# The slot gates' chain moved behind the first expert's w3 products, in both MoE layers

## The chip, the cores and the metric

The kernel runs on one core of a Trainium2 chip. Five engines work from instruction queues of their own and wait for each other through semaphores: the PE (TensorE, matrix products, with weight loads shown apart as PEld), the DVE (VectorE), ACT (ScalarE), POOL (GpSimd) and SP (SyncE, which issues transfers). The metric is the device time of one launch in microseconds (us), and lower is better.

## What is computed

Two layers of a diffusion backbone over 256 latent tokens and 256 context tokens of width 1024, in float32. Each layer ends with a mixture of 16 experts, which is the part that matters here. A router picks two of the 16 experts for each token, and gives it two gate weights:

```python
w = jnp.take_along_axis(scores, expert_idx, axis=-1)
w = w / jnp.sum(w, axis=-1, keepdims=True)
gate = jnp.sum(jax.nn.one_hot(expert_idx, N_EXPERTS) * w[..., None], axis=1)
out = jnp.zeros_like(tok)
for e in range(N_EXPERTS):
    hid = jax.nn.silu(tok @ w1[e]) * (tok @ w3[e])
    out = out + gate[:, e:e + 1] * (hid @ w2[e])
```

w1 and w3 are 1024x512 for each expert, w2 is 512x1024. Layer 0 routes 512 tokens, layer 1 only the 256 latent ones.

## The kernel before

**Slots.** The router sorts the tokens into slots: up to 128 tokens for each expert in layer 0, and for each group of four experts in layer 1. The tables `tok` (which token sits in a slot) and `gw` (its gate weight, a column for each expert) have one row for each slot. `tok` is made at once, since the gathers need it. `gw` is made by a function `R["weights"]()`, which the kernel calls later: a chain of small DVE operations (L972 to L985 in layer 0, L1388 to L1402 in layer 1) that ends in a bf16 table, `wv` or `wb`. Then come small PE products of that table with the one-hot slot matrices (8 in layer 0, `tbw` at L1018; 2 in layer 1, L1430; "the gate product" below) and three DVE operations that add up the parts into `gw`. If an expert or a group had more than 128 tokens, a branch ahead of this would run; it isn't taken with these inputs.

**One expert.** POOL gathers the expert's token rows from memory into a buffer `xg` (there are two, used in turn). The PE transposes them (eight transposes, `tsp`), and ACT and DVE copy the result into two parts, `xh` and `xl`, the value rounded for the PE's fast float32 form and what is left over. Weights come in 1 MB loads into six slots (`raw`); each is split in the same way in two halves, `whi` by ACT (L176) and `wlo` by DVE (L178), into six sets of slots, which are taken again when the PE is through with them. I count these split halves in the order of their use: 1 to 4 are w1 of expert 0, 5 to 8 its w3, 9 and 10 the first half of expert 1's w1, 11 to 14 expert 0's w2, 15 and 16 the second half of expert 1's w1. Every product is then three, hi by hi, hi by lo and lo by hi (`mm3`, L318 to L320), so that a split half feeds six. Of the hidden tiles the DVE makes `g`, which is transposed and split into `gh` and `gl` and multiplied with w2.

**Order.** The code is written expert by expert: the second half of w1, w3 in two halves, the next expert's transposes, `g`, the first half of the next expert's w1, then w2. What stands in each engine's queue is not that order but what a scheduler makes of it when the kernel is built: it plays the program through with costs of its own, and puts an instruction in front of an earlier one where that one would wait. On the chip the queues are then fixed. `issue_after(ins)` keeps the instructions of a block that run on the engine of `ins` behind it in that queue; it sets no wait. `mm_last` is the last PE product that `mm3` has issued.

**Around the change.** In layer 0 the gathers for experts 0 and 1 are issued ahead of the branch, and between them POOL issues four weight loads:

```python
first = self.e_gather(0)
with self.tc.issue_after(first.ins):
    self.ld = nc.gpsimd
    self.prefetch([("moe_w3", (0, 0), 4 * i, 4, 0, 512) for i in range(2)])
    self.prefetch([("moe_w2", (0, 0), 0, 4, 512 * n, 512) for n in range(2)])
    self.ld = nc.sync
    second = self.e_gather(1)
```

All other weight loads go through SP's queue. In layer 1 the first group's tokens are picked by a product on the PE instead of a gather, and four experts share them.

Of the kernel before, what the change touches and what calls it, by code (L numbers as in the profile page):

```python
# [110 lines left out]
class Net:  # L111
# [566 lines left out]
    def moe(self, layer, NT):  # L678
        nc = self.nc
        assert layer == 0  # L680
        with ExitStack() as es:
            rp = self.pool(es, f"moe_r{layer}", 1)
            psp = self.pool(es, f"moe_tp{layer}", 3, space=PSUM)
            hps = self.pool(es, f"moe_h{layer}", 3, space=PSUM)
            yps = self.pool(es, f"moe_y{layer}", 2, space=PSUM)
            fin = [self.ada_mm(1, c, (hps, "h"), psp) for c in self.fill]
            self.prefetch([("moe_w1", (0, 0), 4 * i, 4, 0, 512) for i in range(2)])
            R = self.route(layer, NT, rp, psp)
            with self.tc.issue_after(R["dve"].ins):
                for f in fin:  # L690
                    f()
            self.branch_hint(layer, R)
            self.g2 = [self.mod_bc(rp, layer, G2, i, tag=f"g2{i}") for i in range(NT // 2)]
            ep = self.pool(es, f"moe_e{layer}", 2)
            self.xs = [[ep.tile([128, 8, 128], F32R, name=f"{n}{i}", bufs=1) for n in ("xh", "xl")] for i in range(2)]
            self.facc = ep.tile([128, 2, D], F32, name="facc", bufs=1)
            last = R["dve"]
            after = lambda: (es2.enter_context(self.tc.issue_after(i.ins)) for i in (last, self.rt_act))
            with ExitStack() as es2:
                list(after())  # L700
                xg = self.experts_setup(layer, NT, R, ep, psp, hps, yps)
# [7 lines that stand above are left out]
            with self.tc.issue_after(second.ins):  # L709
                rv = nc.values_load(R["ovf"][0:1, 0:1], min_val=0, max_val=1)  # L710
            self.overflow(rv, self.facc[:, 0], self.facc[:, 1])
            with ExitStack() as es2:
                list(after())
                self.dve_mark, self.act_mark = self.mark()
                es2.enter_context(self.tc.issue_after(self.dve_mark.ins))
                es2.enter_context(self.tc.issue_after(self.zeroed.ins))
                self.act_mark = self.e_tr(0)
                self.e_gather(len(xg))
                self.e_hid(0, "moe_w1", 0)
                R["weights"]()  # L720
                self.expert(0)
            for e in range(1, 16):
                self.expert(e)
            self.hx.close()
            self.moe0_tail(ep, psp, hps)
# [339 lines left out]
    def expert(self, e):  # L1065
        nc, X = self.nc, self.X
        layer, NT, ep, psp, hs, R, T = (X[k] for k in ("layer", "NT", "ep", "psp", "hs", "R", "T"))
        gw = R["gw"][:, e:e + 1]
        self.e_hid(e, "moe_w1", 1)
        self.e_hid(e, "moe_w3", 0)  # L1070
        self.e_tr(e + 1)
        self.e_gather(e + 1 + len(X["xg"]))
        self.e_hid(e, "moe_w3", 1)
        g = ep.tile([128, 512], F32, tag="g", name="g")
        nc.scalar.activation(g, hs[e, "moe_w1"], AF.Silu)
        nc.vector.tensor_tensor(g, g, hs[e, "moe_w3"], ALU.mult)
        gh = ep.tile([128, 4, 128], F32R, tag="gh", name="gh")
        gl = ep.tile([128, 4, 128], F32R, tag="gl", name="gl")
        self.transpose_split(g, 4, gh, gl, psp)
        self.e_hid(e + 1, "moe_w1", 0)  # L1080
        if e < 15:
            y = ep.tile([128, D], F32, tag="y", name="y")
        else:
            S = ep.tile([128, T], F32R, name="S", bufs=1)
            with self.tc.issue_after(self.dve_mark.ins):
                self.onehot(S, NT, R["tokf"][:, e:e + 1])
            yh = ep.tile([128, D], F32R, name="yh", bufs=1)
            yl = ep.tile([128, D], F32R, name="yl", bufs=1)
            X["y"] = S, yh, yl
            wts = [self.weight(("moe_w2", (layer, e), 0, 4, 512 * n, 512)) for n in range(2)]  # L1090
            self.add_sum(2)
        for n in range(2):
            ns = slice(512 * n, 512 * n + 512)
            wt = wts[n] if e == 15 else self.weight(("moe_w2", (layer, e), 0, 4, 512 * n, 512))
            ps = X["yps"].tile([128, 512], F32, tag="y", name="y_ps")
            for k in range(4):
                self.mm3(ps, (gh[:, k], gl[:, k]), self.wk(wt, k), k == 0, k == 3)
            if e < 15:
                nc.scalar.activation(y[:, ns], ps, AF.Copy, scale=gw)  # L1099
            else:  # L1100
                nc.scalar.activation(yh[:, ns], ps, AF.Copy, scale=gw)
                nc.vector.scalar_tensor_tensor(yl[:, ns], ps, gw, yh[:, ns].bitcast(F32), ALU.mult, ALU.subtract)
        if e < 15:
            nc.gpsimd.indirect_dma_start(out=self.F[:, :],  # L1104
                                         out_offset=bass.IndirectOffsetOnAxis(ap=R["tok"][:, e:e + 1], axis=0),
                                         in_=y, in_offset=None, bounds_check=T - 1, oob_is_err=False,
                                         compute_op=ALU.add)
# [352 lines left out]
    def moe1(self):  # L1460
        nc = self.nc
        NT = 2
        with ExitStack() as es:
# [4 lines left out]
            R = self.route1(NT, rp, psp)  # L1468
# [23 lines left out]
            with ExitStack() as es2:  # L1492
                list(after())
                self.dve_mark, self.act_mark = self.mark()
                es2.enter_context(self.tc.issue_after(self.dve_mark.ins))
                self.split_group0(tps)
                for g in range(1, 4):
                    self.gather(xg[g - 1], self.xd, R["tok"][:, g:g + 1], 256)
                self.e_hid(0, "moe_w1", 0)
                R["weights"]()  # L1500
                self.expert1(0)
            for g in range(4):
                nc.gpsimd.memset(hg[g], 0.0)
# [5 lines left out]
    def expert1(self, e):  # L1509
        nc, X = self.nc, self.X  # L1510
        ep, psp, hs, R = (X[k] for k in ("ep", "psp", "hs", "R"))
# [3 lines left out]
        if j == 2 and grp < 3:  # L1515
            xh, xl = X["xs"][(grp + 1) % 2]
            self.transpose_split(X["xg"][grp], 8, xh, xl, psp)
        self.e_hid(e, "moe_w3", 1)
        g = ep.tile([128, 512], F32, tag="g", name="g")
        nc.scalar.activation(g, hs[e, "moe_w1"], AF.Silu)  # L1520
# [196 lines left out]
```

## Time and profile before

| | before |
|---|---|
| device time, three runs | 1286.89, 1287.11, 1289.53 us (median 1287.11) |
| profiled execution, its own time | 1290.84 us |
| its span in the trace | 1289.0 us |
| PE busy | 1203.7 us (93%) |
| DVE busy | 941.8 us (73%) |
| ACT busy | 755.6 us (59%) |
| mean granted clock of the PE | 0.976 of full |
| bytes moved by DMA | 340.60 MB, mean 264 GB/s |

The experts of layer 0 take from about 331 us to 620 us in the span, those of layer 1 from about 978 us to the end. A busy PE is one with a product under way; the granted clock tells at which speed. Products overlap in the pipeline, so the time that one takes away from the next is the distance between two starts and not the duration in the row.

### The profile page before, as it was taken

To read this page: it belongs to the slowest core of one execution; us is meant where nothing else is said; L and a number is where in the kernel's file an instruction comes from. 1 tells how busy PE (TensorE), PEld (TensorE's weight loads), DVE (VectorE), ACT (ScalarE), POOL (GpSimd) and SP (SyncE) were. 2 spreads that over 40 slices of the span, in tenths; PEclk is the share of its full clock that TensorE was granted. 3 is DMA by queue.
4 is the path that set the end of the run, shared out by engine and by line. 5 is a ranking of instruction groups with operands and counts; after the bars stand their busy time and mean duration, and the time that the engine had idled before them with its cause. 6 is when DMAs were issued, how large, how long until landed. Compare 5 with 4: busy or idle time off the path is not lost. (4 is left out here: it accounts for less than half of the span.)

```text
span 1289.0 us, 18819 instructions
## 1 busy us (share of the span) xinstructions
PE 1203.7 (93%) x7093; PEld 946.8 (73%) x7093; DVE 941.8 (73%) x1601; ACT 755.6 (59%) x1122; POOL 124.5 (10%) x126
## 2 busy tenths in 40 slices
PE   4999999898699999999979999999997999999995
PEld 3777666566588888777668888898776788877673
DVE  4755666866698989888897554554657899888985
ACT  3753555723488888778544433343435777777663
POOL 1010102300111112111000000000004000000020
PEclk8999999999799999999989999999998999999998
DMA  9666774342899999999883445432749999889980
GB/s 348 254 238 244 270 256 153 106 166 102 332 354 373 365 363 365 359 362 347 299 326 111 147 157 199 154 119 98 270 174 359 369 369 367 336 334 344 336 335 9
DMA packets 60885, 340.60 MB, mean 264 GB/s; under 512 B 10252, under 2 KB 14860, under 8 KB 24144
## 3 DMA queue, kind: packets, MB, share of 16 engines
q1 hardware_dynamic: 46656, 303.07, 62.4%
q0 software_dynamic: 11392, 31.81, 7.6%
q10 hardware_dynamic: 2736, 4.41, 1.0%
q8 instruction: 59, 0.97, 0.3%
q14 instruction: 42, 0.34, 0.1%
HBM read 333.74 MB, written 18.40 MB: 273 GB/s over the span
## 5 line engine op out<-in xcount | busy, mean ns | idle before, releaser
L178 DVE TENSOR_TENSOR wlo<-raw,whi 128x1024 fp32r<-128x1024 f32 x471 | 558.8, 1221 | 114.2 <-ACT whi L176 113.0
L176 ACT ACTIVATE whi<-raw 128x1024 fp32r<-128x1024 f32 x476 | 481.2, 1054 | 106.8 <-PE qk_ps L319 24.5
L319 PE MATMUL h_ps<-wlo,xh 128*128 128x512 f32 x512 | 208.6, 407 | 4.5 <-DVE wlo L178 4.3
L318 PE MATMUL h_ps<-whi,xh 128*128 128x512 f32 x512 | 206.1, 403 | 3.3 <-ACT xh L1457 2.4
L320 PE MATMUL h_ps<-whi,xl 128*128 128x512 f32 x512 | 206.1, 402 | 0.1
L319 PEld LDWEIGHTS h_ps<-wlo,xh 128*128 128x128 f32 x512 | 97.6, 191 | 38.4 <-DVE wlo L178 17.6
L318 PEld LDWEIGHTS h_ps<-whi,xh 128*128 128x128 f32 x512 | 97.9, 191 | 26.0 <-ACT xh L1457 2.6
L320 PEld LDWEIGHTS h_ps<-whi,xl 128*128 128x128 f32 x512 | 97.6, 191 | 21.3 <-DVE xl L675 0.7
L275 PE MATMUL ada_ps<-raw,cT 128*32 128x128 f32 x1536 | 53.8, 276 | 2.1 <-DMA raw<-in_ada_w 2.1
L319 PE MATMUL y_ps<-wlo,gh 128*128 128x512 f32 (+1 forms) x136 | 53.5, 394 | 0.4 <-DVE wlo L178 0.3
L318 PE MATMUL y_ps<-whi,gh 128*128 128x512 f32 (+1 forms) x136 | 53.0, 391 | 0.7 <-ACT gh L674 0.7
L320 PE MATMUL y_ps<-whi,gl 128*128 128x512 f32 (+1 forms) x136 | 52.6, 395 | 0.1
L275 PEld LDWEIGHTS ada_ps<-raw,cT 128*32 128x32 f32 x1536 | 41.4, 110 | 13.9 <-issue 9.2
L319 PE MATMUL y<-wlo,gh 128*128 128x512 f32 x124 | 49.1, 396 | 0.4 <-DVE wlo L178 0.3
L318 PE MATMUL y<-whi,gh 128*128 128x512 f32 x124 | 49.2, 397 | 0.2 <-ACT gh L674 0.2
L320 PE MATMUL y<-whi,gl 128*128 128x512 f32 x124 | 48.4, 400 | 0.9 <-DVE gl L675 0.8
L1104 POOL DMA_INDIRECT moe_sum<-y,tok x15 | 28.1, 1877 | 158.1 <-ACT y L1099 158.1
L674 ACT ACTIVATE gh<-tsp 128x512 fp32r<-128x512 f32 x32 | 19.1, 596 | 41.4 <-PE tsp L671 41.2
L318 PE MATMUL qk_ps<-xhi,whi 128*128 128x512 f32 x96 | 39.4, 410 | 0.0
L319 PE MATMUL qk_ps<-xlo,whi 128*128 128x512 f32 x96 | 38.7, 403 | 0.0
L320 PE MATMUL qk_ps<-xhi,wlo 128*128 128x512 f32 x96 | 38.3, 399 | 0.0
L1604 POOL DMA_INDIRECT out_dram<-hg,tok x4 | 10.6, 2638 | 268.0 <-DVE hg L1598 218.4
(441 smaller groups left out, 2391.9 us busy)
## 6 DMA issues: line engine op xcount, KB each, us to landing
raw<-in_moe_w SPq DMA_DIRECT2D x188, 1024.0 KB, 7.6
raw<-in_ada_w SPq DMA_DIRECT2D x48, 1024.0 KB, 5.3
raw<-in_ret_w_in SPq DMA_DIRECT2D x24, 1024.0 KB, 5.7
raw<-in_mixab_w_in SPq DMA_DIRECT2D x10, 1024.0 KB, 5.6
raw<-in_ret_w_out SPq DMA_DIRECT2D x8, 1024.0 KB, 4.9
raw<-in_mixab_w_out SPq DMA_DIRECT2D x4, 1024.0 KB, 8.2
raw<-in_moe_w POOLq DMA_DIRECT2D x4, 1024.0 KB, 11.0
bias<-in_rpb ACTq DMA_DIRECT2D x12, 256.0 KB, 5.6
```

Of the source, the lines that this page charges most:

```text
L176: self.nc.scalar.activation(hi, r, AF.Copy)
L178: eng.tensor_tensor(lo, r, hi.bitcast(F32), ALU.subtract)
L275: mm = nc.tensor.matmul(ps[32 * j:32 * j + 32, 0:128], self.cT[:, kk, :], raw[:, k, 128 * j:128 * j + 128], start=(kk == 0), stop=(kk == 7 ...
L318: mm(out, lh, rh, start=first, stop=False)
L319: mm(out, lh, rl, start=False, stop=False)
L320: self.mm_last = mm(out, ll, rh, start=False, stop=last)
L674: i = nc.scalar.activation(hi[:, b0:b0 + w], tv, AF.Copy)
L1104: nc.gpsimd.indirect_dma_start(out=self.F[:, :], out_offset=bass.IndirectOffsetOnAxis(ap=R["tok"][:, e:e + 1], axis=0), in_=y, in_offset=N ...
L1604: self.nc.gpsimd.indirect_dma_start(out=self.out[:, :], out_offset=bass.IndirectOffsetOnAxis(ap=idx, axis=0), in_=x, in_offset=None, bound ...
```

## The change

The call of `R["weights"]()` moves. In layer 0 it stood behind the first half of expert 0's w1 and now stands behind its w3 and expert 1's transposes; in layer 1 it stood at the same place and now stands between the two halves of w3. Its PE products are kept behind the last product that was written before it. Nothing is added and nothing is left out.

```diff
@@ moe, layer 0
                 self.e_hid(0, "moe_w1", 0)
-                R["weights"]()
                 self.expert(0)
@@ expert, layer 0
         self.e_tr(e + 1)
         self.e_gather(e + 1 + len(X["xg"]))
         self.e_hid(e, "moe_w3", 1)
+        if e == 0:
+            with self.tc.issue_after(self.mm_last.ins):
+                R["weights"]()
@@ moe1, layer 1
                 self.e_hid(0, "moe_w1", 0)
-                R["weights"]()
                 self.expert1(0)
@@ expert1, layer 1
+        if e == 0:
+            with self.tc.issue_after(self.mm_last.ins):
+                R["weights"]()
         self.e_hid(e, "moe_w3", 1)
```

The queues of the built kernels show what the scheduler makes of it. The PE's queue at the start of layer 0's experts, before; `xg_3540` and `xh_3535` belong to expert 0, `xg_3541` and `xh_3537` to expert 1, and the first gap holds 45 more products of expert 0:

```order
L671 MATMUL tsp<-cst,xg_3540 128x128 x8
L318 MATMUL h_ps<-whi,xh_3535 128x512
L319 MATMUL h_ps<-wlo,xh_3535 128x512
L320 MATMUL h_ps<-whi,xl_3536 128x512
...
L1018 LDWEIGHTS os_0_3473
L1018 MATMUL tbw<-wv_10198,os_0_3473 128x48
...
L671 MATMUL tsp<-cst,xg_3541 128x128 x8
L318 MATMUL h_ps<-whi,xh_3537 128x512
L319 MATMUL h_ps<-wlo,xh_3537 128x512
L671 MATMUL tsp<-cst,g 128x128 x4
```

The same place of the changed kernel; the gap before the seven transposes holds 33 more products of expert 0, the next one its last 12, and 12 products of expert 1's w1 stand in the third:

```order
L671 MATMUL tsp<-cst,xg_3540 128x128 x8
L318 MATMUL h_ps<-whi,xh_3535 128x512
L319 MATMUL h_ps<-wlo,xh_3535 128x512
L671 MATMUL tsp<-cst,xg_3541 128x128
L320 MATMUL h_ps<-whi,xl_3536 128x512
...
L671 MATMUL tsp<-cst,xg_3541 128x128 x7
...
L318 MATMUL h_ps<-whi,xh_3537 128x512
...
L319 MATMUL h_ps<-wlo,xh_3537 128x512
L1017 LDWEIGHTS os_0_3473
L1017 MATMUL tbw<-wv_10276,os_0_3473 128x48
...
L671 MATMUL tsp<-cst,g 128x128 x4
```

The gate product has moved behind 14 products of expert 1, the last two of which need split half 15. The transposes of expert 1's tokens, which stood behind it, have moved up: the first is now third from expert 0's first product, the other seven stand behind its first half of w3.

The DVE's queue of the changed kernel at the same stretch, from expert 0's last split of w3 (the last of the six) to the left-over part `gl` of expert 0's `g`; the first gap holds the splits 9 and 10 and expert 1's `xl`, the second the splits 12 to 15 with gate operations between them, and the third two more pairs of a one-hot row and a gate addition and the fourth one-hot row:

```order
L178 TENSOR_TENSOR wlo<-raw,whi 128x1024 x6
L971 TENSOR_TENSOR t_0_3466<-of_3442,sc 128x64 x2
...
L1078 TENSOR_TENSOR g<-g,h_ps 128x512
L974 RECIPROCAL one_10262<-one_10262 128x4
L178 TENSOR_TENSOR wlo<-raw,whi 128x1024
...
L984 TENSOR_TENSOR wv_10276<-of_3442,wb_10270 128x8x16
L178 TENSOR_TENSOR wlo<-raw,whi 128x1024
L791 TENSOR_SCALAR S<-cb,tokf_3481 128x128
L1020 COPY gw_3472<-tbw 128x16
...
L675 TENSOR_TENSOR gl<-tsp,gh 128x512
```

Before, the gate operations stood between the splits 2 to 10, the last of them in front of `g` and of all splits of w2; now most of them stand between the splits 11 to 15, behind `g`. The one-hot `S` of expert 15 (four operations) stood some ten splits later.

The PE's queue in layer 1 at the gate product of the changed kernel; `h_ps` are here products of expert 1:

```order
L319 MATMUL h_ps<-wlo,xh_16066 128x512
L1432 LDWEIGHTS os_1_16015
L1432 MATMUL tbw<-wb_17565,os_1_16015 128x48
...
L320 MATMUL h_ps<-whi,xl_16067 128x512
...
L671 MATMUL tsp<-cst,g 128x128 x4
...
L318 MATMUL y_17634<-whi,gh 128x512
L319 MATMUL y_17634<-wlo,gh 128x512
```

The gate product stands seven products later than before (behind the second product of split half 16 and not behind the first of half 15), and the first w2 product (`y`) also has seven more products in front of it than before.

## Rows read from the trace of the kernel before

**Rows 1.** Table of 20-us stretches: busy us of each engine, PEclk, DMA share, GB/s.

```profile
350.00:370.00 20.00, 19.06 (x80) 15.17 (x79) 17.09 (x19) 14.95 (x20) 4.13 (x4) 0.84 0.95 332
370.00:390.00 20.00, 20.00 (x94) 16.20 (x93) 19.21 (x23) 17.10 (x21) 3.67 (x3) 1.00 1.01 370
...
590.00:610.00 20.00, 20.00 (x91) 15.39 (x90) 17.44 (x17) 16.10 (x20) 1.69 (x1) 1.00 1.00 352
```

**Rows 2.** PE timeline, layer 0: start, duration, instruction, [idle before <- releaser].

```profile
332.88 0.79 PE L318 MATMUL h_ps<-whi,xh 128*128 128x512 f32 x1
...
334.06 0.79 PE L320 MATMUL h_ps<-whi,xl 128*128 128x512 f32 x1
...
345.49 0.40 PE L320 MATMUL h_ps<-whi,xl 128*128 128x512 f32 x1
348.79 0.37 PE L1018 MATMUL tbw<-wv,os 128*128 128x48 bf16 x8 [2.91 <-DVE wv L985]
349.13 1.53 PE L671 MATMUL tsp<-cst,xg 128*128 128x128 f32 x8
351.60 0.80 PE L318 MATMUL h_ps<-whi,xh 128*128 128x512 f32 x1 [0.94 <-ACT xh L674]
...
352.62 1.05 PE L671 MATMUL tsp<-cst,g 128*128 128x128 f32 x4
...
354.33 0.63 PE L319 MATMUL h_ps<-wlo,xh 128*128 128x512 f32 x1
354.75 0.63 PE L320 MATMUL h_ps<-whi,xl 128*128 128x512 f32 x1
...
356.44 0.39 PE L318 MATMUL h_ps<-whi,xh 128*128 128x512 f32 x1
356.67 0.40 PE L319 MATMUL h_ps<-wlo,xh 128*128 128x512 f32 x1
...
357.14 0.40 PE L318 MATMUL y_ps<-whi,gh 128*128 128x512 f32 x1
...
368.33 1.03 PE L671 MATMUL tsp<-cst,xg 128*128 128x128 f32 x8
```

**Rows 3.** POOL timeline at the end of layer 0's routing, columns as before.

```profile
326.57 2.17 POOL L157 DMA_DIRECT2D raw<-in_moe_w  x4
329.04 1.05 POOL L1026 DMA_INDIRECT xg<-xd,tok  x1 [0.30 <-issue]
```

**Rows 4.** DMA issues of 328.95 to 331 us: what, median us to landing.

```profile
xg<-xd,tok POOLq DMA_INDIRECT x1, 19.9
```

**Rows 5.** DMA queues, 340 to 349 us: packets, MB, share of 16 engines.

```profile
q1 hardware_dynamic: 424, 3.10, 82.1%
q0 software_dynamic: 193, 0.65, 18.2%
```

**Rows 6.** ACT timeline, layer 0.

```profile
346.23 4.83 ACT L176 ACTIVATE whi<-raw 128x1024 fp32r<-128x1024 f32 x5
350.97 1.07 ACT L674 ACTIVATE xh<-tsp 128x512 fp32r<-128x512 f32 x2
353.71 0.60 ACT L674 ACTIVATE gh<-tsp 128x512 fp32r<-128x512 f32 x1 [1.68 <-PE tsp L671]
355.42 1.06 ACT L176 ACTIVATE whi<-raw 128x1024 fp32r<-128x1024 f32 x1 [1.11 <-PE h_ps L320]
```

**Rows 7.** DVE timeline, layer 0.

```profile
348.45 0.28 DVE L985 TENSOR_TENSOR wv<-of,wb 128x128 bf16<-128x128 f32 x1
...
354.95 4.70 DVE L178 TENSOR_TENSOR wlo<-raw,whi 128x1024 fp32r<-128x1024 f32 x4
```

**Rows 8.** PE timeline, layer 1.

```profile
998.23 0.80 PE L319 MATMUL h_ps<-wlo,xh 128*128 128x512 f32 x1 [2.12 <-DVE wlo L178]
...
1003.44 0.50 PE L318 MATMUL y<-whi,gh 128*128 128x512 f32 x1 [0.22 <-ACT gh L674]
```

**Rows 9.** DVE timeline, layer 1.

```profile
996.97 1.21 DVE L178 TENSOR_TENSOR wlo<-raw,whi 128x1024 fp32r<-128x1024 f32 x1
```

## Prediction

> **What bounds the kernel now.** I read the stretch table first, then the timeline of the PE at the two places where the diff moves something, and last the timelines of the engines and queues that the PE waits for there. In the expert part of layer 0 the table shows the PE busy for all of 20 us at a granted clock of 1.00 in each of the twelve stretches from 370 us to 610 us (the first and the last are in [rows 1]). A product of 128x512 then comes every 0.23 us (356.44 to 356.67), and no later stretch of this part has slack in which a delay could be caught up. So whatever the PE loses at the start of the experts moves the end by as much, and whatever it gains there counts in full.
>
> What it loses there today is in its timeline [rows 2]. The 48 products of expert 0's w1 and w3 run from 332.88 to 345.9. Then the gate product waits 2.91 us for the last gate operation of the DVE. The eight transposes for expert 1 follow at 349.13, there are 0.94 us of waiting for their copy, and expert 1's products start at 351.60 0.42 us apart (354.33 to 354.75), until about 356.4. That is the lower of the PE's two clocks, 1.2 GHz and not 2.4; the stretch from 350 to 370 has a granted clock of 0.84. The products of w2 start at 357.14.
>
> It looks as if the gate chain costs 2.9 us. The second wait is hidden behind it. Expert 1's tokens come by a gather that POOL issues at 329.04, behind four weight loads of 1 MB that it issued from 326.57 [rows 3]; the gather lands 19.9 us after its issue [rows 4], at 348.9. The transposes at 349.13 could not have started before. So the gate product and the transposes become ready within 0.2 us of each other, and taking the gates away would leave the PE at the same place at the same time.
>
> **What the change does, step by step.** The number of instructions is the same; the order is what changes. On the PE in layer 0 the gate product goes behind 14 products of expert 1, as meant. But the transposes for expert 1, which stood behind the gate product, move up with the gap that it left: the first of the eight now stands behind only two of expert 0's products. The PE takes its instructions in order. It gets there at 334.06 (the start of today's third product) and must wait for the gather, with 46 products behind it that ran during the flight until now.
>
> *When the gather lands.* From 340 to 349 us its queue (q0) moves its last 0.65 MB while SP's queue (q1) moves 3.10 MB [rows 5], 0.417 MB per us together. SP loads into a slot when the DVE has split what was in it. Held PE means held slots: the fourth of SP's loads needs splits 7 and 8, which need slots that the stopped products hold. Of the 3.10 MB at most 1.05 MB (one load) is then missing, which is worth 1.05 / 0.417 = 2.5 us at most: landing at 346.4 if all of it was in the gather's way, 348.9 if none. The missing load is the last of the four, so I take 348.0. The Trainium skill, "DMA: Bandwidth & Descriptors", section on queues, rings and completion order, says that each DMA engine takes turns between the queues that have work, a packet at a time. With half of the engines' rate the 0.65 MB would be through at 343.1 in this kernel today, and the change would cost 4.9 us less than I say; the trace has q0 at 18.2% against 82.1%, so equal turns do not give the gather equal bytes.
>
> *From the landing T to the first w2 product, layer 0.*
> - PE: 46 products and 8 transposes. After a wait the products run at 0.43 us for some 4.8 us (351.60 to 356.4): 11 in that time, 35 at 0.233 are 8.2, and the transposes 0.9 (1.03 for eight at 368.33): T + 13.9. ACT's splits fit in: it makes one in 0.97 (4.83 for five), each when the product set six before has freed the slot, as the wait at 355.42 shows [rows 6].
> - DVE: only when w3's products are done can it multiply g (0.6). Behind that stand five weight splits (4.70 for four, so 1.175 each: 5.9) with the gate operations between them, an estimated 1.3 in all (nine, the last 0.28 long, overlapping in part) [rows 7]. The last gate operand is ready at T + 13.9 + 0.6 + 7.2 + 0.2 for the hand-over = T + 21.9. The PE has twelve products of expert 1 and one more to do meanwhile (3 us), and stands for 4 to 5 us. This is a new wait of the kind that the edit was to remove.
> - Then the gate product and the four transposes of g at half clock (1.05 at 352.62) and their copy (0.60 at 353.71): 2.1. The first w2 product comes at T + 24.0.
>
> With T = 348.0 that is 372.0, where today it is 357.14: +14.9. The new order has done 16 of expert 1's w1 products by then, not 12: -0.9. About six w2 products run at half clock after the new wait: +1.1. Sum for layer 0: **+15.1**, with bounds +13.5 (T = 346.4) and +16.0 (T = 348.9). Loads cause no wait of their own: the slots fill while the PE stands.
>
> *Layer 1.* Here the transposes are not touched. The PE waits 2.12 us at 998.23 for one weight split [rows 8], which the DVE starts at 996.97 behind interleaved gate operations [rows 9]. Four of these, an estimated 0.1 us each, move behind it: it starts some 0.3 earlier, and so does the PE. Afterwards the gate product, now behind seven more products, delays the three additions and the next split: the PE waits 0.7 for that split and 0.2 for the copy of g. The first w2 product would come at 1005.4 where it came at 1003.44, with 7 more products behind it (1.6): +0.3. One later split of expert 1's w3 stands one place further back on ACT, which may cost up to 1.2 more, or nothing. Bounds -0.3 and +1.5; I take **+0.5**.
>
> **Sum.** +15.1 + 0.5 = +15.6 us. Against the profiled execution (1290.84 us, span 1289.0) that is 1306.4. It stands 3.7 above the median of the three timed runs, 1287.11, and the sum against that gives 1302.7; I say 1303.
>
> **The rivals.**
> - *The gather lands early.* If the stop on the PE frees the DMA engines far more than by one load, or the two queues share evenly (0.65 MB at half of 0.417 is 3.1 us from 340), T is about 343.1, and the sum is 4.9 less, +10.7: 1298. For it: 0.65 MB is little. Against it: q0's share as above, and three of SP's loads are issued all the same.
> - *The PE isn't held at the transposes,* since they are passed or the tokens are there at 334. The 48 products and the transposes are then done at 346.8, but the copies for expert 1 stand behind three splits on ACT (2.9 us from 346.23, and 1.07 for the copies) and end at 350.2; its products run at half clock to 354.9; the DVE's row of five splits begins at 351.1, and 7.8 later the last gate operand comes, at 358.9, the first w2 product at 361.0. With the -0.9 and +1.1 of above that is +4.0 in layer 0, so 1291.6. The Trainium skill, "TensorE: Matmul & The Clock Gate", in its table of specifications, says that TensorE's queue reorders in part, pulling weight loads ahead of products that are under way; read as letting ready products past, it would give this time. The trace speaks against that reading: during the 2.12 us wait of 998.23 the next product, whose operands were there, did not run.
> - *Faster.* The wait of 2.91 at the gate product goes, with the 0.94 behind it, and the half clock after it (11 products at 0.19 more: 2.1), and nothing takes its place: 1287.1 - 5.9 = 1281. It decides itself at one point, the last gate operand: it must be ready when the PE has done 62 products, near 350. Today it is ready at 348.7, with the splits of w2 behind it; in the new order they stand in front.
> - *A longer hold.* On the DVE the four one-hot operations of expert 15 come up in front of the gate additions and of the copy that the w2 products need. In the built program the first of them waits for a transfer on POOL's queue. If that is expert 3's gather, which can be issued some 13 us after T when its buffer is transposed, and it takes 19.9 us like the one before, it holds the DVE until T + 33 and not T + 23 or so, the w2 products 9 us longer: 1312.
> - *Nothing,* within 0.2%: some of the above cancel. No single row gives it.
>
> That the change doesn't take effect is excluded by the order rows.
>
> **How the numbers follow.** My forecast, T between 346.4 and 349: 0.70. Early gather 0.10, PE not held 0.07, faster 0.04, longer hold 0.06, nothing 0.03. The first two lie in 1297 to 1308, with 2 us for the half-clock stretches and layer 1 on either side; that leaves 0.20 out. A difference of 0.2% (2.6 us) is about what a measurement of this kernel tells from none. Faster by more than that 0.04, within it 0.03, slower 0.93.
>
> **What would show it.** In the timeline of the changed kernel: two products, then a PE wait of 12 to 15 us that ends with the transfer of expert 1's tokens; a second one of 4 to 5 us before the gate product, ended by the DVE; the first w2 product at 370 to 373; nearly the same busy stretches after it, some 15 us later; and in layer 1 less than 2 us either way. The prediction is wrong if the first transposes run at 334, if the second wait is missing, or if a later stretch of layer 0 makes up for several us, which would mean that the PE was not the bound there.

## The result and the profile after

The changed kernel takes **1304.66 us** (median of three runs, 1303.7 to 1306.42), where the kernel before took 1287.11. The ratio is 1.0128, with an interval of 1.0114 to 1.0143, so 14.7 to 18.4 us more. The forecast was 1303. The profiled execution took 1304.66 us, span 1302.8.

The table of 20-us stretches of the changed kernel, with the columns of [rows 1], shows where the time goes. The first stretch has 12 PE instructions, transposes among them, where the stretch from 330 to 350 of the kernel before had 70; from 390 on the PE is again busy for all of each stretch until 630.

```profile
330.00:350.00 20.00, 3.53 (x12) 2.63 (x13) 8.34 (x9) 3.09 (x4) 0.00 (x0) 0.50 0.87 361
...
390.00:410.00 20.00, 20.00 (x94) 16.09 (x93) 18.63 (x20) 16.82 (x21) 3.15 (x2) 1.00 1.00 359
```

The PE's timeline of the changed kernel, layer 0, is the answer to [rows 2]:

```profile
330.80 1.94 PE L671 MATMUL tsp<-cst,xg 128*128 128x128 f32 x8 [5.37 <-DMA xg<-xd,tok]
332.58 0.79 PE L318 MATMUL h_ps<-whi,xh 128*128 128x512 f32 x1
333.17 0.63 PE L319 MATMUL h_ps<-wlo,xh 128*128 128x512 f32 x1
349.47 0.45 PE L671 MATMUL tsp<-cst,xg 128*128 128x128 f32 x1 [15.67 <-DMA xg<-xd,tok]
349.57 0.78 PE L320 MATMUL h_ps<-whi,xl 128*128 128x512 f32 x1
...
362.91 0.39 PE L320 MATMUL h_ps<-whi,xl 128*128 128x512 f32 x1
...
370.75 0.58 PE L319 MATMUL h_ps<-wlo,xh 128*128 128x512 f32 x1 [4.39 <-DVE wlo L178]
371.13 0.54 PE L1017 MATMUL tbw<-wv,os 128*128 128x48 bf16 x8
...
373.28 0.79 PE L318 MATMUL y_ps<-whi,gh 128*128 128x512 f32 x1
...
384.17 1.03 PE L671 MATMUL tsp<-cst,xg 128*128 128x128 f32 x8
```

Two products run, then one transpose waits 15.67 us for expert 1's tokens, and the product behind it (349.57), whose operands are those of the two before and their left-over part, waits with it. The last of expert 0's 48 products starts at 362.91. The second wait, 4.39 us, stands one product ahead of the gate product and is for a weight split (`wlo`), not for a gate operand; the gate product runs right behind it. At equal work, 24 w2 products and 36 of expert 1, the next transposes start at 384.17, 53.37 us after the first ones at 330.80. Before, these were 368.33 and 331.10 [rows 2], 37.23 us apart. So layer 0 loses **16.1 us** by there.

The DVE's timeline of the changed kernel shows the second wait from the other side. The operations from L971 to L984 are the gates.

```profile
352.75 1.23 DVE L178 TENSOR_TENSOR wlo<-raw,whi 128x1024 fp32r<-128x1024 f32 x1 [14.11 <-ACT whi L176]
...
363.34 0.69 DVE L1078 TENSOR_TENSOR g<-g,h_ps 128x512 f32<-128x512 f32 x1
...
367.71 0.28 DVE L984 TENSOR_TENSOR wv<-of,wb 128x128 bf16<-128x128 f32 x1
...
369.48 1.22 DVE L178 TENSOR_TENSOR wlo<-raw,whi 128x1024 fp32r<-128x1024 f32 x1
370.61 0.28 DVE L984 TENSOR_TENSOR wv<-of,wb 128x128 bf16<-128x128 f32 x1
370.81 1.22 DVE L178 TENSOR_TENSOR wlo<-raw,whi 128x1024 fp32r<-128x1024 f32 x1
```

The DVE stood for 14.11 us as well, because no split slot came free: ACT, which makes the other half of each split first, waited for the PE to get through with the set in use (ACT's timeline of the changed kernel):

```profile
351.66 1.06 ACT L176 ACTIVATE whi<-raw 128x1024 fp32r<-128x1024 f32 x1 [16.39 <-PE h_ps L320]
```

From `g` on the DVE works without a gap, and the split that ends at 370.7 is the one for which the PE waits; the last gate operand follows 0.2 us later, while the PE is in that product.

In layer 1 the PE's timeline of the changed kernel answers to [rows 8]:

```profile
994.42 0.50 PE L318 MATMUL h_ps<-whi,xh 128*128 128x512 f32 x1 [3.50 <-ACT xh L1459]
...
1013.40 0.50 PE L319 MATMUL h_ps<-wlo,xh 128*128 128x512 f32 x1 [2.19 <-DVE wlo L178]
1013.74 0.39 PE L320 MATMUL h_ps<-whi,xl 128*128 128x512 f32 x1
...
1017.24 0.50 PE L319 MATMUL h_ps<-wlo,xh 128*128 128x512 f32 x1 [0.64 <-issue]
...
1019.56 0.50 PE L318 MATMUL y<-whi,gh 128*128 128x512 f32 x1
```

### The profile page after: what moved, and what is told of

It is laid out like the page before. It is cut to its first block, busy times and chain, and to the rows that moved or that the text cites. A ratio compares the mean times of both kernels' runs of the same rounds, so it can differ in the third digit from the quotient of the medians.

```text
span 1302.8 us, 18824 instructions
## 1 busy us (share of the span) xinstructions
PE 1202.7 (92%) x7093; PEld 946.4 (73%) x7093; DVE 942.3 (72%) x1601; ACT 756.3 (58%) x1122; POOL 125.2 (10%) x126
## 5 line engine op out<-in xcount | busy, mean ns | idle before, releaser
L319 PEld LDWEIGHTS h_ps<-wlo,xh 128*128 128x128 f32 x512 | 97.1, 190 | 41.6 <-DVE wlo L178 20.1
L671 PE MATMUL tsp<-cst,xg 128*128 128x128 f32 x152 | 22.5, 281 | 21.0 <-DMA xg<-xd,tok 21.0
```

Source lines behind the costliest of these rows:

```text
L319: mm(out, lh, rl, start=False, stop=False)
L671: nc.tensor.transpose(tp[:, 128 * b:128 * b + 128], src[:, 128 * (b0 + b):128 * (b0 + b) + 128], self.ident)
```

## The experiments

Eleven kernels, in three sets; each set has runs of the kernel before of its own, with medians of 1288.62, 1287.54 and 1287.37 us (single runs from 1283.6 to 1293.4).

**E1: the hold without the gates' move.** Layer 1 as before; in layer 0 only expert 1's transposes are written earlier.

```diff
@@ before: moe
                 self.e_hid(0, "moe_w1", 0)
+                self.e_tr(1)
+                self.e_gather(3)
                 R["weights"]()
@@ expert
-        self.e_tr(e + 1)
-        self.e_gather(e + 1 + len(X["xg"]))
+        if e:
+            self.e_tr(e + 1)
+            self.e_gather(e + 1 + len(X["xg"]))
```

> Before, with one thing changed in layer 0: expert 1's transposes are written ahead of the gates, so that the PE's queue has the first of them behind two of expert 0's products, as in the changed kernel; the gates stay early on the DVE, ahead of g, and layer 1 is as before. Theory of the prediction (the hold at the transposes is the larger half, the gates behind the splits the smaller): the PE waits 15 to 16 us for the gather at the third product, there is no second wait of 4 us, the first w2 product comes near 368, and the time is 1297 to 1300. Rival (the gates' place on the DVE makes most of the cost): 1287 to 1292. Rival (the hold makes all of it): 1303 to 1305.

Measured: 1299.59, ratio 1.0082 (1.006 to 1.0103), so 11.0 us more than before by the medians, 7.7 to 13.3 by the interval. The PE's timeline of E1 has the first wait, a little shorter than the 15 to 16 us expected, and no other behind it:

```profile
347.13 0.45 PE L671 MATMUL tsp<-cst,xg 128*128 128x128 f32 x1 [14.12 <-DMA xg<-xd,tok]
...
364.72 0.41 PE L318 MATMUL y_ps<-whi,gh 128*128 128x512 f32 x1
```

By the medians the hold, without a gate moved, makes about two thirds of the loss (11.0 of 17.55). Both rivals are out.

**E2: the gates' move without the hold.** The changed kernel, with expert 1's transposes kept behind expert 0's last product.

```diff
@@ after: expert
-        self.e_tr(e + 1)
-        self.e_gather(e + 1 + len(X["xg"]))
+        if e:
+            self.e_tr(e + 1)
+            self.e_gather(e + 1 + len(X["xg"]))
         self.e_hid(e, "moe_w3", 1)
+        if e == 0:
+            with self.tc.issue_after(self.mm_last.ins):
+                self.e_tr(1)
+            self.e_gather(3)
         if e == 0:
             with self.tc.issue_after(self.mm_last.ins):
                 R["weights"]()
```

> The changed kernel with expert 1's transposes in layer 0 kept behind expert 0's last w3 product on the PE; everything else is written as in the change. Theory (hold at the transposes): the 48 products run from 333 to 346 during the gather's flight, the PE then waits some 3 us for the gather at 349, the gates' row on the DVE is done before split 15 is needed or within 2 us of it, and the time is 1287 to 1292. Rival (the gates behind the splits set the time): the second wait of 4.4 us stays and grows, 1300 or more.

Measured: 1291.32, ratio 1.0026 (1.0013 to 1.0038), 2.7 us more than before. The PE's timeline of E2:

```profile
345.93 1.35 PE L671 MATMUL tsp<-cst,xg 128*128 128x128 f32 x8 [3.59 <-DMA xg<-xd,tok]
348.27 0.80 PE L318 MATMUL h_ps<-whi,xh 128*128 128x512 f32 x1 [1.00 <-ACT xh L674]
354.99 0.50 PE L319 MATMUL h_ps<-wlo,xh 128*128 128x512 f32 x1 [1.10 <-DVE wlo L178]
```

The gather is waited for all the same, but behind 48 products and for 3.59 us. The gates behind the splits cost 1.10 here and 4.39 in the changed kernel. The row on the DVE is no shorter; its timeline of E2, from `g` to split half 15:

```profile
346.42 0.66 DVE L1083 TENSOR_TENSOR g<-g,h_ps 128x512 f32<-128x512 f32 x1
...
353.71 1.23 DVE L178 TENSOR_TENSOR wlo<-raw,whi 128x1024 fp32r<-128x1024 f32 x1
```

That is 8.5 us, against 7.4 in the changed kernel (363.34 to 370.7). But the PE comes to the product that needs this split 7.5 us after the start of `g` (at 353.89). The waits of 3.59 and 1.00 have put expert 1's first product behind `g` (348.27), and most of the thirteen up to there run at half clock. In the changed kernel expert 1's first product starts just ahead of `g` (363.14), and the PE comes there 3.0 us after the start of `g`.

So the two parts don't simply add. Measured in the profiles from expert 0's first transposes to the last transposes of a `g` in layer 0, the kernel before takes 297.65 us and E9 below, whose layer 0 is the same, 296.99; E1 is 9.9 above the former, E2 1.5, and the changed kernel 15.6 (E10 below, with the same layer 0, 16.5).

**E3: the gather issued earlier.** The changed kernel; on the engines' queues nothing but POOL's order differs.

```diff
@@ after: moe
             with self.tc.issue_after(first.ins):
+                second = self.e_gather(1)
+            with self.tc.issue_after(second.ins):
                 self.ld = nc.gpsimd
...
+                fourth = self.ld_last
                 self.ld = nc.sync
-                second = self.e_gather(1)
-            with self.tc.issue_after(second.ins):
+            with self.tc.issue_after(fourth.ins):
```

> The changed kernel with one thing moved: POOL issues expert 1's gather right behind expert 0's, ahead of the four weight loads of 1 MB and not behind them; the queues of PE, DVE and ACT are the same word for word. Theory (the PE waits for the landing of that gather, which is late because it stands behind the loads): the gather lands within 6 us of its issue or so, by 334, the wait at the third product falls from 15.7 us to 0 to 2, and the time is 1285 to 1291, 14 to 20 us less than the changed kernel. Rival (the gather is slow by itself, about 20 us whatever stands ahead of it): it lands at 346 to 347 and the time is 1301 to 1303.

Measured: 1291.95, ratio 1.0033 (1.001 to 1.0055): 3.3 us above before, where the changed kernel was 17.55 above. The rows of expert 1's gather, from the DMA issues of the changed kernel (328.5 to 332 us) and of E3 (323.5 to 332 us), last number median us to landing:

```profile
xg<-xd,tok POOLq DMA_INDIRECT x1, 20.5
```

```profile
xg<-xd,tok POOLq DMA_INDIRECT x1, 5.4
```

Issued ahead of the loads the transfer takes 5.4 us; the other 15 come from the four loads ahead of it and from SP's loads, which share the DMA engines while it waits. No run tells these two apart. In E3's PE timeline the hold is gone and other waits remain:

```profile
346.79 0.80 PE L318 MATMUL h_ps<-whi,xh 128*128 128x512 f32 x1 [3.40 <-ACT xh L674]
...
355.45 0.49 PE L319 MATMUL h_ps<-wlo,xh 128*128 128x512 f32 x1 [4.02 <-DVE wlo L178]
```

So the landing of this gather is what the PE waited for in the first wait. The second needs no hold: the wait of 4.02 us is there with the PE running, as the gates stand behind the splits here too, and the PE comes to the split 3.4 us after the start of `g` (348.05 to 351.43). The time is 1 us above the stated band: waits of 7.42 us are left where the kernel before has 3.85 (2.91 and 0.94). The copies for expert 1, the wait of 3.40, stand on ACT behind split half 9, whose load ACT gets 12.6 us after the first transposes, as late as in E2, where the gather stands behind the loads.

**E4: gates early, only the gate product late, gather early.** The changed kernel, with E3's edit; in layer 0 the DVE's part of `weights()` is called where it was before, and only `slot_weights` behind w3.

```diff
@@ after: weights()
-        def weights():
+        def weights(late=False):
...
-            return self.slot_weights(NT, R, psp, R["gw"], oslot)
+            if not late:
+                return self.slot_weights(NT, R, psp, R["gw"], oslot)
@@ moe
                 self.e_hid(0, "moe_w1", 0)
+                R["weights"](True)
@@ expert
         if e == 0:
             with self.tc.issue_after(self.mm_last.ins):
-                R["weights"]()
+                self.slot_weights(NT, R, psp, R["gw"], R["oslot"])
```

> Layer 0: the gates' operations stay early on the DVE, as before the change, only the gate product goes behind expert 0's w3 products; expert 1's gather is issued ahead of the four loads. Layer 1 as in the change. Theory: neither the wait of 2.91 us for the last gate operand nor a hold at the transposes is left, nor the 0.94 behind it, and the time is 1281 to 1284, below the kernel before. Rival (the splits of w2 or the loads, delayed by the gather, become the next wait of the same size): 1286 to 1290.

Measured: 1288.44, ratio 0.9994 (0.9983 to 1.0005): no gain, the rival's band. The PE's timeline of E4 at the gate product:

```profile
353.30 0.50 PE L1021 MATMUL tbw<-wv,os 128*128 128x48 bf16 x8 [5.76 <-DVE wv L987]
```

The last gate operand comes later still. On the DVE it stands behind the left-over part of expert 1's tokens, which waits for ACT's copies (DVE timeline of E4):

```profile
352.35 0.69 DVE L675 TENSOR_TENSOR xl<-tsp,xh 128x512 fp32r<-128x512 f32 x1 [3.64 <-ACT xh L674]
352.96 0.28 DVE L987 TENSOR_TENSOR wv<-of,wb 128x128 bf16<-128x128 f32 x1
```

Why no gain appeared is the question of the next four kernels.

**E5, E6, E7: one of the pair, the other, both.** The prediction said that before the change the gate product and the gather came due together, so that taking away one would change nothing. E5 is the kernel before with E3's edit. E6 is the kernel before with E2's edit of the transposes and, on the DVE, the gates in one block ahead of the third split:

```diff
@@ before: weights(), moe
-                V.tensor_tensor(wv[:, :, :, j], of, wb[:, j, :, :, None].to_broadcast([128, 2, NT, 16]), ALU.mult)
+                R["wl"] = V.tensor_tensor(wv[:, :, :, j], of, wb[:, j, :, :, None].to_broadcast([128, 2, NT, 16]), ALU.mult)
...
-                self.expert(0)
+                with self.tc.issue_after(R["wl"].ins):
+                    self.expert(0)
```

E7 has the edits of both.

> Before, with expert 1's gather issued right behind expert 0's and ahead of the four weight loads; the order on PE, DVE and ACT is that of before. Theory (before, gate product and gather came due within 0.2 us of each other, so taking away one of the two changes nothing): the gate product still waits about 3 us for its last operand, the transposes follow it at once, and the time is within 1.5 us of before. Rival (the gather alone held the PE before): 1283 to 1285.

> Before, with the gates' operations of layer 0 in one block on the DVE ahead of the third weight split, so that the gate product goes behind 14 products of expert 0 without a wait; expert 1's transposes are kept behind expert 0's last w3 product, and its gather stays behind the loads. Theory (the other half of the pair): the wait of 2.9 us moves from the gate product to the transposes, which wait 3 to 4 us for the gather, and the time is within 1.5 us of before. Rival (the gates alone held the PE): 1281 to 1285.

> Both of the former together: gates in one block ahead of the third split, and expert 1's gather ahead of the loads, its transposes behind expert 0's last w3 product. Theory: neither wait is left and the time is 2 to 5 us below before, 1283 to 1286. Rival (the weight loads and their splits stand right behind the two and take over): within 1 us of before.

Measured: E5 1290.94, ratio 1.0018 (1.0004 to 1.0032); E6 1286.68, ratio 0.9986 (0.9971 to 1.0001); E7 1289.22, ratio 1.0009 (0.9991 to 1.0026). The PE's waits around layer 0's first experts (us in total, times, longest), of E5 and then of E6:

```profile
PE tsp L671 <- DMA xg<-xd,tok: 4.8, 1, 4.8
PE h_ps L318 <- ACT xh L674: 3.0, 1, 3.0
PE tbw L1020 <- DVE wv L987: 2.9, 1, 2.9
```

```profile
PE tsp L671 <- DMA xg<-xd,tok: 7.2, 2, 5.4
PE h_ps L318 <- ACT xh L674: 0.9, 1, 0.9
```

With the gather early, the gate product still waits 2.9 and the copies cost 3.0 instead of 0.94 [rows 2]. With the gates early, the gate wait is gone and the transposes wait 1.85 (7.2 less the 5.4 of expert 0's), where 3 to 4 were expected. Each half of the pair holds when the other is taken away, as the prediction said; E5 is even slower, by 2.3 us after its ratio and 3.4 by the medians, so outside its band of 1.5. But E7, where both are gone, gains nothing either, and its rival holds in the time: its PE waits 1.4 us for `g`, 1.8 for expert 1's copies and 0.8 for a split, 3.9 in all, as long as before. What stands behind the two is in ACT's timeline, of the kernel before (the row ahead of [rows 6]) and then of E7:

```profile
343.37 1.06 ACT L176 ACTIVATE whi<-raw 128x1024 fp32r<-128x1024 f32 x1 [4.68 <-DMA raw<-in_moe_w]
```

```profile
340.31 1.06 ACT L176 ACTIVATE whi<-raw 128x1024 fp32r<-128x1024 f32 x1 [1.37 <-DMA raw<-in_moe_w]
...
343.18 4.83 ACT L176 ACTIVATE whi<-raw 128x1024 fp32r<-128x1024 f32 x5
347.92 1.07 ACT L674 ACTIVATE xh<-tsp 128x512 fp32r<-128x512 f32 x2
```

In both, ACT waits for the first load of expert 1's w1, makes split half 9 of it and then five more splits, and only then the copies of expert 1's tokens. These start 19.7 us after expert 0's first transposes in E7 and 19.9 before (350.97), with the tokens and the gates early or not. This is the third wait behind the two. In E5 the copies start at 21.8, as ACT waits 1.36 us for one more load there.

**E8: everything early.** E7, with expert 1's transposes written as in E1 and not behind w3.

> As the former, and expert 1's transposes are written right behind expert 0's, so that they, their copies on ACT and their left-over parts on the DVE stand ahead of the splits of w3 and w2. Theory: expert 1's products find their operands ready, the half clock behind the waits goes too, and the time is 3 to 6 us below before, 1282 to 1285. Rival (loads and splits take over): within 1 us of before.

Measured: 1289.58, ratio 1.0006 (0.9993 to 1.0018): no gain. The PE's and then ACT's timeline of E8:

```profile
343.50 0.79 PE L318 MATMUL h_ps<-whi,xh 128*128 128x512 f32 x1 [4.33 <-ACT whi L176]
```

```profile
334.42 2.01 ACT L176 ACTIVATE whi<-raw 128x1024 fp32r<-128x1024 f32 x2 [2.19 <-DMA raw<-in_moe_w]
338.90 2.00 ACT L176 ACTIVATE whi<-raw 128x1024 fp32r<-128x1024 f32 x2 [2.47 <-DMA raw<-in_moe_w]
...
342.39 1.06 ACT L176 ACTIVATE whi<-raw 128x1024 fp32r<-128x1024 f32 x1 [0.52 <-DMA raw<-in_moe_w]
```

The PE now waits 4.33 us for a split. In E8's built queue the product that waits is `h_ps<-whi,xh_3537`, one of expert 1, which the scheduler has put behind only 20 of expert 0's 48 products; its split is half 9 (342.39), and ACT waited for loads three times on the way there. So with its tokens early, a product of expert 1 has risen in the queue and holds 28 of expert 0's behind it, the same kind of hold as in the changed kernel. E8 therefore doesn't show what the kernel would gain with all three waits away, and no other run does.

**E9, E10: the two layers apart.** E9 is the change in layer 1 alone, E10 that in layer 0 alone.

> The change in layer 1 alone, layer 0 as before. The prediction: 0.5 us slower than before (-0.3 to +1.5). Theory after the trace of the changed kernel (the same wait of about 2 us stays, but without the half clock behind it, and later splits come out 0.4 to 1 us better): 0.5 to 1.7 us faster than before.

> The change in layer 0 alone, layer 1 as before. The prediction: 15.1 us slower than before, half a us less than the whole change. Theory after the trace: 16 to 17.5 us slower than before, as slow as the whole change or up to 1.5 us slower.

Measured: E9 1287.99, ratio 1.0004 (0.9993 to 1.0016); E10 1306.06, ratio 1.0138 (1.0118 to 1.0158), 15.2 to 20.3 us (18.7 by the medians, above the 16 to 17.5 of my theory). The whole loss is layer 0's. In layer 1 my theory of a gain of 0.5 to 1.7 us is not borne out. The profiles say why it looked so. After the wait of 2.12 us the kernel before ran eight products at half clock (998.23 to 1001.38, 0.43 us apart), the changed kernel none. But E10, whose layer 1 is that of before, has the same wait and none either (PE timeline of E10):

```profile
1013.57 0.50 PE L319 MATMUL h_ps<-wlo,xh 128*128 128x512 f32 x1 [2.12 <-DVE wlo L178]
1013.90 0.40 PE L320 MATMUL h_ps<-whi,xl 128*128 128x512 f32 x1
1014.13 0.39 PE L318 MATMUL h_ps<-whi,xh 128*128 128x512 f32 x1
```

From layer 1's first product to the PE's last one, the old order takes 294.32 us before and 294.28 in E5, with the half clock, and 292.85 in E10 and 292.86 in E6, without it. The new order takes 294.05 in E3 and 293.96 in E4 with it, and 292.61, 292.58 and 292.68 in the changed kernel, E9 and E11 without. At the same clock the new order is worth -0.2 to -0.3 us.

**E11: E6 with the change of layer 1.**

> The best of the layer 0 orders (gates in one block ahead of the third split, transposes behind expert 0's last w3 product, gather behind the loads) with the change of layer 1. If the gains add up: 2 to 3.5 us below before. Rival (both gains are below what can be measured): within 1 us of before.

Measured: 1287.76, ratio 0.9997 (0.9985 to 1.0009). The rival: no version here is measurably faster than the kernel before.

## Why the prediction was right

**The bound.** That a delay at the start of the experts is not caught up was right: in the changed kernel the view of the PE's waits between 370 and 640 lists the 4.39 us and nothing else, and the last transposes of a `g` in layer 0 come 313.2 us after the first transposes (644.00 and 330.80), where these were 297.65 apart (628.75 and 331.10). Of 16.1 us 15.6 are still there.

**The first wait** was the main step, and it was right: two products, then a wait ended by expert 1's tokens. It is 15.67 us where 12 to 15 were said. E3 shows the cause by taking it away, E1 its size. The rival that the transposes would be passed is out: the ready product at 349.57 stood behind the transpose. So is the longer hold: the one-hot operations of expert 15 run on the DVE from 371.95 without a wait. The specification in the Trainium skill, "TensorE: Matmul & The Clock Gate", that was weighed there speaks of weight loads alone; the trace gives no case of a product that passes another.

**The landing T** was mis-sized. I took 348.0, since a load that SP could not issue would leave its bytes to the gather. From 340 to 349 us q1 did move less, 2.26 MB and not 3.10 [rows 5], but the gather landed at 349.4 (18.6 us after expert 0's transposes, 17.8 before). The stretches of the changed kernel's DMA queues from 340 to 346.4 and from 346.4 to 349.4 show that bytes were not what it lacked at the end:

```profile
q1 hardware_dynamic: 271, 1.95, 72.9%
q0 software_dynamic: 195, 0.75, 28.7%
```

```profile
q1 hardware_dynamic: 53, 0.32, 25.7%
q0 software_dynamic: 16, 0.04, 3.5%
```

In the last 3 us q0 has 16 packets left and the engines are 29% busy, and still it takes them 3 us. In the kernel before, q0's last 15 packets and 0.04 MB take the 2.5 us up to its landing (346.4 to 348.9), with q1 at 97.1%. What makes these last packets slow no run here tells. So the premise of this step, that fewer bytes of SP's bring the gather forward, failed: T is 1.4 us later than I took, 1.7 counted from expert 0's first transposes, and beyond the 348.9 that I had as its bound. The rival of an early landing (343.1, equal turns of the queues) is out with it: while both queues had work, q0 had 28.7% against 72.9%. The Trainium skill, "DMA: Bandwidth & Descriptors", section on queues, rings and completion order, has the engines change queues after a packet; it states no equal shares of bytes, and the trace has none.

**From T on** the sum held: the last product of expert 0 at T + 13.5 (start; 13.9 said for its end), the last gate operand at T + 21.5 (21.9), the first w2 product at T + 23.9 (24.0). The second wait is 4.39 us (4 to 5 said) and ended by the DVE. Only its name was wrong: the split of half 15 came due before the last gate operand. The half clock behind it held for two w2 products and not six: the 1.1 us counted for it were about 0.6 (from the first w2 product to the next transposes 10.89 us, 11.19 before, with four products fewer, 0.9). These errors, T too early and the half clock too long, partly cancel: the sum of +15.1 for layer 0 stands against 16.1 measured.

**Layer 1** was said to cost 0.5 us. Its steps came as told (counted from the first product the split is there 0.4 earlier, a new wait of 0.64, the first w2 product 25.14 us after the first product and not 24.56), and the sum of them is not measurable.

**What the profile alone could not settle:** the two profiled executions differ by 13.8 us (1290.84 and 1304.66), the medians by 17.55. The profile of before was 3.7 above its median, and held the half clock in layer 1, 1.4 us. The traces account for 15.6 to 16.1 us in layer 0 and the timed runs say 14.7 to 18.4; where in that range the change lies is not settled closer.

**The pair before** (gates and gather within 0.2 us of each other) was right as far as each holds the PE without the other. That removing both would gain (the rival "faster", 1281) had a third wait behind it that I had priced only under another rival: ACT's copies of expert 1's tokens, behind splits that wait for a load (E7).

## What to carry to other kernels

When an instruction moves back in a queue that is taken in order, look at what moves up into its place and at what that waits for: here the waiting product was cheap, and what rose into its gap was a transpose whose tokens were 15 us away. An instruction that depends on a transfer belongs behind the work that covers the flight. Before a wait is removed, find the one that would end next, and the one after that. Here three of different engines came due within 3 us of each other in the kernel before (the last gate operand at 348.7, the tokens at 348.9, ACT's copies at 351.6), and taking away two of them gained nothing that can be measured.

## What had not been expected of the hardware

A gather took 5.4 us behind another gather (E3) and 20.5 us behind four loads of 1 MB on its queue (the changed kernel), with SP's loads beside it. Its last 16 packets took 3 us there with the DMA engines 29% busy, and its last 15 took 2.5 us in the kernel before with them nearly fully busy. The clock after the same wait of some 2.1 us in layer 1 was half for some 3 us in four profiles (before, E3, E4, E5) and full in the other nine, in both orders of the instructions: 1.4 us between two profiles that the order of layer 1's instructions doesn't explain.
